# PSUM and probability tiles of two banks for both heads and for two GLA token tiles, in a two-layer hybrid encoder

## The chip, the cores and the metric

The kernel runs on one core of one Trainium2 chip. The metric is the device time of one execution in microseconds (us): 1145.85 is the median of three runs of the kernel before (1144.88 to 1146.09). Everything is float32 or the same numbers in the rounded form fp32r. The five engines of the core work side by side, each through its own list of instructions in order: TensorE (PE) multiplies matrices into PSUM, VectorE (DVE) and ScalarE (ACT) work on SBUF and PSUM, GpSimd (POOL) on a few tiles, and SyncE (SP) issues the DMAs. PSUM has eight banks; one bank holds 512 float32 columns on 128 partitions.

## The reference

512 tokens of width 1024 pass through two layers. Each layer normalizes, multiplies by one wide input projection, and divides its columns among three mixers: gated linear attention (GLA, 4 heads), a convolution module with 31 taps, and attention with a bias (6 heads of 64). Their outputs are concatenated, projected and added; then comes an MLP with a squared ReLU. Cut to what matters here:

```python
kv = jnp.einsum('bnchk,bnchv->bnhkv', k_dec, vf)      # GLA, one product per chunk of 64
def step(state, inp):
    a, kv_c = inp
    state = a[..., None] * state + kv_c
    return state, state
_, states = lax.scan(step, init, (chunk_decay, kv))   # 8 chunks in sequence
o = jnp.einsum('bnchk,nbhkv->bnchv', qf, states)
o = o * lax.rsqrt(jnp.mean(o * o, axis=-1, keepdims=True) + EPS)
...
scores = einsum('bnqhd,bnkhd->bnhqk', qc, k_band) * (ATT_HEAD_DIM ** -0.5)
p = jax.nn.softmax(jnp.where(valid, scores + bias, NEG_INF), axis=-1)
o = einsum('bnhqk,bnkhd->bnqhd', p, v_band)
...
h = h + mixed @ w_out[l]
h = h + sq_relu_mlp(rmsnorm(h, norm_ffn[l]), w_up[l], w_down[l])
```

## The kernel before

Activations lie transposed: 128 of the 1024 features on the partitions, 512 tokens along the free axis. Each operand of a large product is split in two fp32r numbers, high and low, and each product is three matmuls (lines 165 to 167): high by high, high by low, low by high. The weights arrive by DMA as float32; ACT makes the high part (L126), DVE the low part (L127).

A layer runs as follows. First the convolution's three projections `cv`, then the group `in_0`. Then comes a list of units (near line 803): projections of attention's queries and keys (`in_3` to `in_8`), of GLA's queries (`in_1`, `in_2`), and three token groups `tb`, `ta`, `tc` in which the tokens lie on the partitions (lines 465 to 467). After each unit's pieces, which count as so many microseconds of products, the table PACE advances three side tasks by a rate: attention (`att_steps`), GLA (`gla_steps`) and the convolution. The side tasks are generators; each `yield` is a step. Next is the output projection in two parts (`op`), beside the first of which attention and GLA go on; then the MLP (`up`, `dn`). So the order of the program text, and a scheduler's choice by priority, sets where a side task's matmuls stand between the dense ones on PE.

Attention works on pairs of heads. For head pair `pr` the steps are: scores of query tiles 0 and 1, scores of tile 2, transposes of 0 and 1, scores of 3, transposes of 2, values of 0 and 1, transposes of 3, values of 2 and 3. The scores (`sc`, L679) of each head have their own PSUM bank of the tag "at" (three buffers): head `s` uses rows 64·s to 64·s + 63 of the array. `softmax` adds the bias and takes the maximum on DVE (`mx`, L692), then the exponential and the scaling on ACT, into the probability tile `sn`. `turn` transposes `sn` on PE (`pt`, L711), into another bank of "at", and ACT copies it to `ps`. `values` multiplies it with the values (`ao`, L722), 64 columns of the array for each head, also in "at". The projections `in_3` and `in_4` and small norms take "at" too.

```python
BANKS = {"mm": 3, "at": 3, "gc": 2}
for step, *idx in (
    (scores, (0, 1)), (scores, (2,)), (turns, 0, 1), (scores, (3,)), (turns, 2),
    (attended, 0, 1), (turns, 3), (attended, 2, 3),
):
```

GLA and the convolution share the tag "gc" (two banks). `gz` (L501) and `gx` make the gates; `kv` (L544) is the product of keys and values for two token tiles, 64 rows by 64 columns of the array for each; DVE carries the state on from chunk to chunk (`st`); `go` (L583) multiplies the queries by the states, for one token tile at a time; ACT copies it out, DVE normalizes it, and `gla_out` transposes it (`ot`, L621).

## Time and profile before

| | |
|---|---|
| median of three runs | 1145.85 us (1144.88 to 1146.09) |
| the profiled execution | 1146.69 us |
| its span, from first to last instruction | 1144.9 us |
| busy of the span: PE, its weight loads, DVE, ACT, POOL | 99%, 81%, 55%, 43%, 2% |
| mean granted clock of PE | 0.997 |
| read from HBM | 105.22 MB |

The profiled execution is longer than its span by 1.8 us, which lie around it. The profile's times are of this one execution. The start and the busy time of each instruction are shown by the timeline; the matmuls of a pipelined engine overlap there, so that the distance from one start to the next, not a matmul's own duration, tells what it occupies. A plain float32 matmul such as `go` or `kv` stands there as two, so x16 are eight of the program.

### The profile page before, as it was taken

What the parts mean: (1) busy time and instruction counts of PE and PEld (TensorE: products, weight loads), DVE (VectorE), ACT (ScalarE), POOL (GpSimd) and SP (SyncE); (2) the same over time, 40 slices, a digit from 0 to 9 for tenths busy, and PEclk for the clock granted to TensorE, in tenths of its full rate; (3) what the DMA queues carried; (4) which work ended last, traced back from release to release, by engine and by line L of the source; (5) the groups of instructions that cost most, each with busy time, mean ns of one, the idle gap of its engine ahead of it and who ended that gap; (6) DMA issues with size and microseconds to landing.
All of it is one profiled execution on the core that took longest, in us unless ns stands there. A gap on an engine that the chain in (4) does not pass through costs nothing.

```text
span 1144.9 us, 14044 instructions
## 1 busy us (share of the span) xinstructions
PE 1131.3 (99%) x5552; PEld 929.5 (81%) x5552; DVE 628.2 (55%) x1041; ACT 488.8 (43%) x843; POOL 20.9 (2%) x39
## 2 busy tenths in 40 slices
PE   9999999999999999999999999999999999999996
PEld 7888878888888888888888788788888888888885
DVE  7897786743433344334359957867434333443344
ACT  6454795634311243333243567845343112433222
POOL 0000010000000000000000000100000000000002
PEclk9999999999999999999999999999999999999998
DMA  8231312232223223332242321222332232223312
GB/s 282 94 106 51 97 56 74 95 106 94 92 92 109 94 92 94 107 112 81 77 132 90 104 60 38 93 74 92 103 100 92 92 105 97 92 93 99 104 37 74
DMA packets 34657, 108.21 MB, mean 95 GB/s; under 512 B 4256, under 2 KB 7456, under 8 KB 34592
## 3 DMA queue, kind: packets, MB, share of 16 engines
q1 hardware_dynamic: 34592, 107.33, 28.9%
q8 instruction: 43, 0.70, 0.3%
q14 instruction: 22, 0.18, 0.0%
HBM read 105.22 MB, written 2.10 MB: 94 GB/s over the span
## 4 chain that ended last, share of the span: by engine, by line
PE 97%; DVE 1%; DMA 1%; ACT 0%; issue 0%; DVEq 0%; SPq 0%; ACTq 0%
PE dn L167 10%; PE dn L166 10%; PE dn L165 10%; PE up L166 10%; PE up L165 10%; PE up L167 10%; PE in L165 3%; PE op L165 3%; PE op L166 3%; PE in L167 3%; PE in L166 3%; PE op L167 3%; PE sc L679 2%; PE ao L722 1%; PE pt L711 1%; PE cv L165 1%
## 5 line engine op out<-in xcount | busy, mean ns | idle before, releaser
L126 ACT CAST h_w<-r_w 128x1024 fp32r<-128x1024 f32 x146 | 153.8, 1053 | 443.8 <-PE dn L166 216.8
L127 DVE TENSOR_TENSOR l_w<-r_w,h_w 128x1024 fp32r<-128x1024 f32 x146 | 178.4, 1223 | 300.2 <-ACT h_w L126 299.4
L165 PE MATMUL dn<-uh,h_w 128*128 128x512 f32 (+1 forms) x528 | 202.7, 384 | 0.0
L167 PE MATMUL dn<-uh,l_w 128*128 128x512 f32 (+1 forms) x528 | 202.5, 383 | 0.0
L166 PE MATMUL dn<-ul,h_w 128*128 128x512 f32 (+1 forms) x528 | 202.4, 383 | 0.0
L166 PEld LDWEIGHTS dn<-ul,h_w 128*128 128x128 f32 x528 | 99.2, 188 | 20.0
L165 PEld LDWEIGHTS dn<-uh,h_w 128*128 128x128 f32 x528 | 99.2, 188 | 19.9
L167 PEld LDWEIGHTS dn<-uh,l_w 128*128 128x128 f32 x528 | 99.2, 188 | 19.8
L872 DVE TENSOR_TENSOR dt<-dn,n2r 128x512 f32<-128x512 f32 (+1 forms) x33 | 22.3, 675 | 115.0 <-PE dn L167 115.0
L382 DVE SCALAR_TENSOR_TENSOR acc<-hp,cl,acc 128x512 f32<-128x512 f32 x120 | 82.1, 745 | 0.1
L862 DVE TENSOR_TENSOR ul<-ur,uh 128x512 fp32r<-128x512 f32 x64 | 44.4, 693 | 2.1
L857 ACT ACTIVATE ur<-ur 128x512 f32<-128x512 f32 x64 | 40.6, 634 | 1.9
L856 ACT ACTIVATE ur<-up 128x512 f32<-128x512 f32 x64 | 37.8, 590 | 0.0
L697 ACT ACTIVATE sn<-sn,mx 128x128 f32<-128x128 f32 (+3 forms) x48 | 26.6, 554 | 9.7 <-DVE mx L692 9.4
L702 ACT ACTIVATE sn<-sn,ri 128x128 f32<-128x128 f32 (+3 forms) x48 | 26.8, 559 | 6.4 <-DVE ri L701 6.2
L861 DVE CAST uh<-ur 128x512 fp32r<-128x512 f32 x64 | 27.3, 427 | 0.0
L793 DVE TENSOR_TENSOR hT<-hT,op 128x512 f32<-128x512 f32 x32 | 21.9, 683 | 6.4 <-PE op L167 6.2
L167 PE MATMUL up<-x_0h,l_w 128*128 128x512 f32 x64 | 24.9, 389 | 0.0
L165 PE MATMUL up<-x_2h,h_w 128*128 128x512 f32 x64 | 24.9, 389 | 0.0
L165 PE MATMUL up<-x_0h,h_w 128*128 128x512 f32 x64 | 24.9, 389 | 0.0
L166 PE MATMUL up<-x_0l,h_w 128*128 128x512 f32 x64 | 24.9, 389 | 0.0
L165 PE MATMUL up<-x_1h,h_w 128*128 128x512 f32 x64 | 24.9, 389 | 0.0
(814 smaller groups left out, 2387.3 us busy)
## 6 DMA issues: line engine op xcount, KB each, us to landing
r_w<-in_wm SPq DMA_DIRECT2D x146, 512.0 KB, 3.5
r_wo<-in_wo SPq DMA_DIRECT2D x16, 512.0 KB, 3.6
r_tb<-in_wtb SPq DMA_DIRECT2D x8, 480.0 KB, 4.2
r_ta<-in_wta SPq DMA_DIRECT2D x8, 480.0 KB, 4.3
ab<-in_relx SPq DMA_DIRECT2D x12, 256.0 KB, 4.3
r_tc<-in_wtc SPq DMA_DIRECT2D x8, 384.0 KB, 3.3
r_wc<-in_wc SPq DMA_DIRECT2D x6, 384.0 KB, 4.6
hT<-in_xT SPq DMA_DIRECT2D x8, 256.0 KB, 5.5
```

What stands on the lines that cost most here:

```text
L126: nc.scalar.copy(out=hi, in_=raw)
L127: nc.vector.tensor_tensor(out=lo, in0=raw, in1=hi.bitcast(F32), op=ALU.subtract)
L165: nc.tensor.matmul(out=ps, lhsT=hi[:, sl], rhs=xh, start=first and i == 0, stop=False)
L166: nc.tensor.matmul(out=ps, lhsT=hi[:, sl], rhs=xl, start=False, stop=False)
L167: nc.tensor.matmul(out=ps, lhsT=lo[:, sl], rhs=xh, start=False, stop=last and i == n - 1)
L382: nc.vector.scalar_tensor_tensor(out=acc[c], in0=hp[c][:, j : j + T], scalar=weight(c, j), in1=acc[c], op0=ALU.mult, op1=ALU.add,)
L697: nc.scalar.activation(out=sn[:, 0:n], in_=sn[:, 0:n], func=AF.Exp, scale=-1.0, bias=mx, accum_out=sm)
L702: nc.scalar.activation(out=sn[:, 0:n], in_=sn[:, 0:n], func=AF.Copy, scale=ri)
L856: nc.scalar.activation(out=r, in_=ps, func=AF.Relu)
L857: nc.scalar.activation(out=r, in_=r, func=AF.Square)
L861: nc.vector.tensor_copy(out=hi, in_=r)
L862: nc.vector.tensor_tensor(out=lo, in0=r, in1=hi.bitcast(F32), op=ALU.subtract)
```

## The change

Scores, transposes and probabilities of both heads of a pair now share tiles of two banks, [128, 2, 512]: one PSUM buffer "at" of two banks in place of three of one, in SBUF two tiles each for `sn` and `ps` in place of five. `ao` gets a bank of its own, which `in_0` uses too. `in_3` and `in_4` are the two banks of one tile `in_34`. "gc" becomes one buffer of two banks. Copies of transposes take both heads, and for query tiles 0 and 1 all four parts, in one ACT instruction. GLA works on two token tiles at a time: the states of four chunks, then sixteen matmuls `go`, then one normalization of both and six transposes into one tile. Two rates of PACE differ. In the MLP the pairs `uh`, `ul` that lived in `sn` and `ps` tiles lie in one such tile. The diff, cut to its core:

```diff
-BANKS = {"mm": 3, "at": 3, "gc": 2}
+ROOM = {"s": 38, "cv": 8, "sn": 2, "ps": 2, "bias": 4, "os": 3}
+BANKS = {"mm": 3, "ao": 1, "at": 1, "gc": 1}
...
-    (0.4, 0.75, 0.6),
-    (0.3, 0.35),
+    (0.4, 0.65, 0.6),
+    (0.3, 0.2),
...
-    def at_ps(name):
-        return mm_ps(name, "at")
+    def two_heads(name, pool=pp, tag="at", dt=F32):
+
+        return pool.tile([P, 2, T], dt, tag=tag, bufs=(BANKS if pool is pp else ROOM)[tag], name=name)
 
     def gc_ps(name):
-        return mm_ps(name, "gc")
+        return two_heads(name, tag="gc")[:, 0, :]
...
-        psb.append(in_group(0, at_ps))
+        psb.append(in_group(0, lambda name: mm_ps(name, "ao")))
...
-                pk = [gc_ps(f"kv{l}_{i}_{h}") for h in range(2)]
+                pk = two_heads(f"kv{l}_{i}", tag="gc")
...
-            for t in range(NT):
-                if t % 2 == 0:
-                    kvs = chunk_products(t // 2)
...
+            for i in range(2):
+                kvs = chunk_products(i)
+                yield True
                 sts = []
-                for h in range(2):
-                    n = 2 * t + h
-                    pk = kvs[h]
-                    c0 = 2 * (t % 2) * GDV
-                    cur = sp.tile([P, 2 * GDV], F32, tag="st", bufs=4, name=f"st{l}_{n}")
+                for n in range(4 * i, 4 * i + 4):
+                    pk = kvs[:, n % 2, (n // 2 % 2) * 2 * GDV :]
...
-                o = s_tile(f"os{l}_{t}")
-                ov = o[:, 0:384].rearrange("p (a b d) -> p a b d", b=2, d=GDV)
-                pos = [gc_ps(f"go{l}_{t}_{hh}") for hh in range(2)]
-                for pr in range(2):
-                    for hh in range(2):
-                        rr = slice(hh * GP, (hh + 1) * GP)
-                        for h in range(2):
-                            n = 2 * t + h
-                            nc.tensor.matmul(
-                                out=pos[hh][h * CHUNK : (h + 1) * CHUNK, pr * GDV : (pr + 1) * GDV],
-                                lhsT=qT[pr][rr, n * CHUNK : (n + 1) * CHUNK],
-                                rhs=sts[h][rr, pr * GDV : (pr + 1) * GDV], start=True, stop=True,
-                            )
-                for hh in range(2):
+                yield True
+                o = sp.tile([P, 2, 384], F32, tag="os", bufs=ROOM["os"], name=f"os{l}_{i}")
+                go = two_heads(f"go{l}_{i}", tag="gc")
+                for t in range(2):
+                    for pr in range(2):
+                        c0 = (2 * t + pr) * GDV
+                        for hh in range(2):
+                            rr = slice(hh * GP, (hh + 1) * GP)
+                            for h in range(2):
+                                n = 4 * i + 2 * t + h
+                                nc.tensor.matmul(
+                                    out=go[h * CHUNK : (h + 1) * CHUNK, hh, c0 : c0 + GDV],
+                                    lhsT=qT[pr][rr, n * CHUNK : (n + 1) * CHUNK],
+                                    rhs=sts[2 * t + h][rr, pr * GDV : (pr + 1) * GDV],
+                                    start=True, stop=True,
+                                )
+                for t in range(2):
                     nc.scalar.copy(
...
-                sq = s_tile(f"oq{l}_{t}")
-                nc.scalar.activation(out=sq[:, 0:384], in_=o[:, 0:384], func=AF.Square)
-                vs = small([P, GH], f"ov{l}_{t}")
+                flat = o.rearrange("p t d -> p (t d)")
+                sq = sp.tile([P, 2 * 384], F32, tag="os", bufs=ROOM["os"], name=f"oq{l}_{i}")
+                nc.scalar.activation(out=sq, in_=flat, func=AF.Square)
+                vs = small([P, 2 * GH], f"ov{l}_{i}")
                 nc.vector.reduce_sum(
-                    out=vs, in_=sq[:, 0:384].rearrange("p (h d) -> p h d", d=GDV), axis=AX.X
+                    out=vs, in_=sq.rearrange("p (h d) -> p h d", d=GDV), axis=AX.X
                 )
...
-        def gla_out(o_s, t):
-            o = o_s[t]
-            nc.vector.tensor_tensor(
-                out=o[:, 0:384], in0=o[:, 0:384], in1=gates[t][:, 0:384], op=ALU.mult
-            )
-            pt = gc_ps(f"ot{l}_{t}")
-            for f in range(3):
-                nc.tensor.transpose(
-                    out=pt[:, f * P : (f + 1) * P], in_=o[:, f * P : (f + 1) * P], identity=ident
-                )
-            ts = slice(t * P, (t + 1) * P)
-            if t == 0:
+        def gla_out(o_s, i):
+            o = o_s[i]
...
+            for j in range(2):
+                t = 2 * i + j
+                nc.vector.tensor_tensor(
+                    out=o[:, j, :], in0=o[:, j, :], in1=gates[t][:, 0:384], op=ALU.mult
+                )
+                for f in range(3):
+                    fc = slice(f * P, (f + 1) * P)
+                    nc.tensor.transpose(out=pt[:, j, fc], in_=o[:, j, fc], identity=ident)
+            ts = slice(2 * i * P, 2 * (i + 1) * P)
...
             for f, (hi, lo) in enumerate(gmx):
-                src = pt[:, f * P : (f + 1) * P]
-                nc.scalar.copy(out=hi[:, ts], in_=src)
-                nc.vector.tensor_tensor(
-                    out=lo[:, ts], in0=src, in1=hi.bitcast(F32)[:, ts], op=ALU.subtract
-                )
+                src = pt[:, :, f * P : (f + 1) * P]
+                hi3, lo3 = (a[:, ts].rearrange("p (j t) -> p j t", t=P) for a in (hi, lo))
+                nc.scalar.copy(out=hi3, in_=src)
+                nc.vector.tensor_tensor(out=lo3, in0=src, in1=hi3.bitcast(F32), op=ALU.subtract)
```

```diff
@@ attention
-                pss = [at_ps(f"sc{l}_{2 * pr + s}_{idx[0]}") for s in range(2)]
+                pss = two_heads(f"sc{l}_{pr}_{idx[0]}")
+                probs[idx[-1]] = two_heads(f"sn{l}_{pr}_{idx[0]}", sp, "sn")
...
                     for s in range(2):
-                        softmax(i, s, pss[s][:, (i - idx[0]) * 2 * P :])
-
-            def softmax(i, s, psc):
+                        softmax(i, s, pss[:, s, (i - idx[0]) * 2 * P :], probs[idx[-1]][:, s, (i - idx[0]) * P :])
+
+            def softmax(i, s, psc, sn):
...
-            def turn(i, s):
-                n = (i + 1) * P
-                nm_ = f"{l}_{2 * pr + s}_{i}"
-                sn = probs[i, s]
-                pt = at_ps(f"pt{nm_}")
-                for j in range(i + 1):
-                    nc.tensor.transpose(
-                        out=pt[:, j * P : (j + 1) * P], in_=sn[:, j * P : (j + 1) * P], identity=ident
-                    )
-                p_ = room("ps", i, s)
-                nc.scalar.copy(out=p_[:, 0:n], in_=pt[:, 0:n])
-                pts[i, s] = p_
+
+            def turns(*idx):
+                nm_ = f"{l}_{pr}_{idx[0]}"
+                sn = probs[idx[-1]]
+                pt = two_heads(f"pt{nm_}")
+                n = 0
+                for i in idx:
+                    for s in range(2):
+                        for j in range(i + 1):
+                            cc = slice(n + j * P, n + (j + 1) * P)
+                            nc.tensor.transpose(out=pt[:, s, cc], in_=sn[:, s, cc], identity=ident)
+                    n += (i + 1) * P
+                p_ = two_heads(f"ps{nm_}", sp, "ps")
+                nc.scalar.copy(out=p_[:, :, 0:n], in_=pt[:, :, 0:n])
+                at = 0
+                for i in idx:
+                    pts[i] = p_[:, :, at * P : (at + i + 1) * P]
+                    at += i + 1
...
-                    pos.append(at_ps(f"ao{l}_{pr}"))
+                    pos.append(mm_ps(f"ao{l}_{pr}", "ao"))
...
+            both = two_heads(f"in{l}_34") if pr == 0 else None
             for i in range(2):
                 yield from in_pieces(
-                    3 + 2 * pr + i, lambda ps: att_evac(pr, i, ps), at_ps if pr == 0 else mm_ps
+                    3 + 2 * pr + i, lambda ps: att_evac(pr, i, ps),
+                    mm_ps if pr else lambda name: both[:, i, :],
...
-                tags = places[i]
-                hi = s_tile(f"uh{l}_{f}", F32R, tags)
-                lo = s_tile(f"ul{l}_{f}", F32R, tags)
+                if places[i] in ("sn", "ps"):
+                    both = two_heads(f"uhl{l}_{f}", sp, places[i], F32R)
+                    hi, lo = both[:, 0, :], both[:, 1, :]
+                else:
+                    hi = s_tile(f"uh{l}_{f}", F32R, places[i])
+                    lo = s_tile(f"ul{l}_{f}", F32R, places[i])
```

How this changes the order on PE, at three places of the first layer (line numbers are each kernel's own).

PE, from the projection `in_3` (weights `h_w_3`, `l_w_3`) on, before and after; `tb0p` is the first tile of the token group `tb`.

```order
L166 MATMUL in_3_368<-x_7l,h_w_3_363 128x512
L167 MATMUL in_3_368<-x_7h,l_w_3_364 128x512
L165 MATMUL in_4_411<-x_0h,h_w_4_406 128x512
L166 MATMUL in_4_411<-x_0l,h_w_4_406 128x512
L167 MATMUL in_4_411<-x_0h,l_w_4_407 128x512
L165 MATMUL in_4_411<-x_1h,h_w_4_406 128x512
```

```order
L167 MATMUL in_34_362<-x_7l,h_w_3_364 128x512
L168 MATMUL in_34_362<-x_7h,l_w_3_365 128x512
L466 MATMUL tb0p_467<-h_tb_0_444,x_0h 128x480
L467 MATMUL tb0p_467<-l_tb_0_445,x_0h 128x480
...
L467 MATMUL tb0p_467<-l_tb_1_451,x_2h 128x480
L468 MATMUL tb0p_467<-h_tb_1_450,x_2l 128x480
L166 MATMUL in_34_362<-x_0h,h_w_4_406 128x512
L167 MATMUL in_34_362<-x_0l,h_w_4_406 128x512
```

Before, `in_4` follows at once, in another bank; after, nine matmuls of `tb` stand between the two halves of `in_34`.

PE, where the scores of query tile 2 of the first head pair stand; `sc_0_2` and `sc_1_2` are heads 0 and 1 before, and `sc_0_2` is both heads after.

```order
L167 MATMUL in_6_700<-x_5h,l_w_6_696 128x512
L679 MATMUL sc_0_2_721<-qk_0_1h,qk_0_0h 128x384
L679 MATMUL sc_1_2_722<-qk_0_1h,qk_0_0h 128x384
L679 MATMUL sc_0_2_721<-qk_0_1h,qk_0_0l 128x384
L679 MATMUL sc_1_2_722<-qk_0_1h,qk_0_0l 128x384
L679 MATMUL sc_0_2_721<-qk_0_1l,qk_0_0h 128x384
L679 MATMUL sc_1_2_722<-qk_0_1l,qk_0_0h 128x384
L165 MATMUL in_6_700<-x_6h,h_w_6_695 128x512
```

```order
L168 MATMUL in_6_696<-x_7h,l_w_6_692 128x512
L166 MATMUL in_1_759<-x_0h,h_w_1_754 128x512
L167 MATMUL in_1_759<-x_0l,h_w_1_754 128x512
L675 MATMUL sc_0_2_717<-qk_0_1h,qk_0_0h 128x384 x2
L675 MATMUL sc_0_2_717<-qk_0_1h,qk_0_0l 128x384 x2
L675 MATMUL sc_0_2_717<-qk_0_1l,qk_0_0h 128x384 x2
L168 MATMUL in_1_759<-x_0h,l_w_1_755 128x512
```

The group moved from before `in_6`'s sixth matmul from the end to behind the second of the next projection, `in_1`: eight dense matmuls later.

PE, the last `go` of the layer, before (beside the scores of heads 4 and 5) and after; `st` are the states, `gq` the queries.

```order
L167 MATMUL op_0_0_1813<-mc_1h,l_wo_0_0_1809 128x512
L679 MATMUL sc_4_3_1827<-qk_2_1h,qk_2_0h 128x512
L679 MATMUL sc_4_3_1827<-qk_2_1h,qk_2_0l 128x512
L679 MATMUL sc_4_3_1827<-qk_2_1l,qk_2_0h 128x512
L583 MATMUL go_3_0_1858<-st_6_1851,gq_0_809 64x96
L583 MATMUL go_3_0_1858<-st_7_1854,gq_0_809 64x96
L583 MATMUL go_3_1_1859<-st_6_1851,gq_0_809 64x96
L679 MATMUL sc_5_3_1828<-qk_2_1h,qk_2_0h 128x512
L679 MATMUL sc_5_3_1828<-qk_2_1h,qk_2_0l 128x512
L679 MATMUL sc_5_3_1828<-qk_2_1l,qk_2_0h 128x512
L583 MATMUL go_3_1_1859<-st_7_1854,gq_0_809 64x96
L583 MATMUL go_3_0_1858<-st_6_1851,gq_1_848 64x96
```

```order
L466 MATMUL tc0p_1673<-h_tc_2_1334,x_4h 128x384
L582 MATMUL go_1_1681<-st_4_1661,gq_0_797 64x96
L582 MATMUL go_1_1681<-st_5_1664,gq_0_797 64x96
L582 MATMUL go_1_1681<-st_4_1661,gq_0_797 64x96
L582 MATMUL go_1_1681<-st_5_1664,gq_0_797 64x96
...
L582 MATMUL go_1_1681<-st_6_1667,gq_0_797 64x96
L582 MATMUL go_1_1681<-st_7_1670,gq_0_797 64x96
...
L582 MATMUL go_1_1681<-st_7_1670,gq_1_836 64x96
L467 MATMUL tc0p_1673<-l_tc_2_1335,x_4h 128x384
```

Before, the eight matmuls of token tile 3 are cut by the scores of head 5, and those of tile 2 stand in two places ahead of them. After, sixteen matmuls of token tiles 2 and 3 are one run among dense matmuls of `tc`.

## Rows read from the trace of the kernel before

**Rows 1.** The page, busy time: us, share of the span, instructions, by engine.

```profile
PE 1131.3 (99%) x5552; PEld 929.5 (81%) x5552; DVE 628.2 (55%) x1041; ACT 488.8 (43%) x843; POOL 20.9 (2%) x39
```

**Rows 2.** The page, the chain that ended last, share by engine.

```profile
PE 97%; DVE 1%; DMA 1%; ACT 0%; issue 0%; DVEq 0%; SPq 0%; ACTq 0%
```

**Rows 3.** Stretches: us, busy us (instructions) of PE, PEld, DVE, ACT, POOL; PEclk, DMA share, GB/s.

```profile
28.00:112.00 84.00, 84.00 (x423) 68.81 (x423) 72.36 (x121) 41.34 (x79) 1.10 (x5) 1.00 0.27 88
112.00:172.00 60.00, 60.00 (x443) 47.69 (x442) 46.51 (x120) 50.29 (x121) 3.02 (x3) 1.00 0.23 74
674.00:734.00 60.00, 60.00 (x443) 47.69 (x441) 46.67 (x120) 50.45 (x121) 3.02 (x3) 1.00 0.22 73
1120.00:1145.00 25.00, 13.69 (x105) 12.65 (x103) 12.44 (x22) 6.84 (x16) 7.40 (x9) 0.84 0.25 84
```

**Rows 4.** Timeline, PE, dense products: start, us, engine, line, operation, out<-in, count [wait].

```profile
36.90 0.39 PE L167 MATMUL in<-x_7h,l_w 128*128 128x512 f32 x1
37.13 0.39 PE L165 MATMUL in<-x_0h,h_w 128*128 128x512 f32 x1
```

**Rows 5.** Timeline, PE: a run of scores among dense products.

```profile
68.74 0.39 PE L167 MATMUL in<-x_7h,l_w 128*128 128x512 f32 x1
...
69.64 0.28 PE L679 MATMUL sc<-qk_1h,qk_0l 64*128 64x256 f32 x2
69.76 0.28 PE L679 MATMUL sc<-qk_1l,qk_0h 64*128 64x256 f32 x2
...
70.30 0.40 PE L166 MATMUL in<-x_0l,h_w 128*128 128x512 f32 x1
```

**Rows 6.** Timeline, PE: a run of `go` of x16.

```profile
151.59 0.44 PE L467 MATMUL tc0p<-h_tc,x_7l 128*128 128x384 f32 x1
151.96 0.56 PE L583 MATMUL go<-st,gq 64*64 64x96 f32 x16
...
152.73 0.34 PE L466 MATMUL tc0p<-l_tc,x_0h 128*128 128x384 f32 x1
```

**Rows 7.** Timeline, PE: a run of `go` of x8.

```profile
162.50 0.33 PE L467 MATMUL tc0p<-h_tc,x_3l 128*128 128x384 f32 x1
...
162.85 0.34 PE L466 MATMUL tc0p<-l_tc,x_4h 128*128 128x384 f32 x1
163.12 0.55 PE L583 MATMUL go<-st,gq 64*64 64x96 f32 x8
...
163.88 0.33 PE L465 MATMUL tc0p<-h_tc,x_5h 128*128 128x384 f32 x1
```

**Rows 8.** Timeline, PE: `go` inside a group of scores.

```profile
169.34 0.40 PE L167 MATMUL op<-mc_1h,l_wo 128*128 128x512 f32 x1
...
170.56 0.39 PE L583 MATMUL go<-st,gq 64*64 64x96 f32 x6
...
171.77 0.54 PE L583 MATMUL go<-st,gq 64*64 64x96 f32 x10
...
172.58 0.40 PE L166 MATMUL op<-ma_0l,h_wo 128*128 128x512 f32 x1
```

**Rows 9.** Timeline, DVE: it reads the product `in_3`.

```profile
38.33 0.68 DVE L649 SCALAR_TENSOR_TENSOR aq<-in,n_0rb 128x512 f32<-128x512 f32 x1
```

**Rows 10.** Timeline, PE, second layer: the scores wait for DVE.

```profile
635.19 0.44 PE L679 MATMUL sc<-qk_1h,qk_0h 64*128 64x384 f32 x1
636.20 0.41 PE L679 MATMUL sc<-qk_1h,qk_0h 64*128 64x384 f32 x1 [0.57 <-DVE mx L692]
```

**Rows 11.** Timeline, DVE: the last maximum of the second head pair's first group.

```profile
120.12 0.08 DVE L692 DVE_READ_ACCUMULATOR2_ANT mx<- 128x1 f32 x1
```

**Rows 12.** Timeline, PE: `gz` beside it.

```profile
119.63 0.92 PE L501 MATMUL gz<-wg,gq 128*128 128x256 f32 x3
```

**Rows 13.** Timeline, PE, near the start.

```profile
9.61 0.63 PE L165 MATMUL cv<-x_1h,h_wc 128*128 128x512 f32 x1
10.04 0.63 PE L166 MATMUL cv<-x_1l,h_wc 128*128 128x512 f32 x1
```

More of the change, by code (lines that the diff above doesn't have):

```diff
@@ L169, in col_sums @@
     def col_sums(src, name, w=ones):
-        pc = at_ps(f"{name}pc")
+        pc = gc_ps(f"{name}pc")
         for j in range(NT):
@@ L204, in bcast @@
             )
-        pb = at_ps(f"{name}pb")
+        pb = gc_ps(f"{name}pb")
         nc.tensor.matmul(out=pb, lhsT=ones, rhs=dg, start=True, stop=True)
@@ L253, in encoder_kernel @@
     nc.vector.tensor_copy(out=ones_r, in_=ones)
-    warm = at_ps("warm")
+    warm = gc_ps("warm")
     for i in range(NWARM):
@@ L544, in chunk_products @@
                                 nc.tensor.matmul(
-                                    out=pk[h][hh * GP : (hh + 1) * GP, c0 : c0 + GDV],
+                                    out=pk[hh * GP : (hh + 1) * GP, h, c0 : c0 + GDV],
                                     lhsT=kd[i][rows, o0 : o0 + GP],
@@ L551, in gla_states @@
             prev = None
-            for t in range(NT):
-                if t % 2 == 0:
-                    kvs = chunk_products(t // 2)
-                    yield True
+            for i in range(2):
+                kvs = chunk_products(i)
+                yield True
                 sts = []
-                for h in range(2):
-                    n = 2 * t + h
-                    pk = kvs[h]
-                    c0 = 2 * (t % 2) * GDV
-                    cur = sp.tile([P, 2 * GDV], F32, tag="st", bufs=4, name=f"st{l}_{n}")
+                for n in range(4 * i, 4 * i + 4):
+                    pk = kvs[:, n % 2, (n // 2 % 2) * 2 * GDV :]
+                    cur = sp.tile([P, 2 * GDV], F32, tag="st", bufs=6, name=f"st{l}_{n}")
                     if n == 0:
@@ L604, in gla_states @@
                 yield True
-                r = rsqrt(GH, f"on{l}_{t}", v=vs)
-                for g in range(GH):
-                    gc = slice(g * GDV, (g + 1) * GDV)
+                r = rsqrt(2 * GH, f"on{l}_{i}", v=vs)
+                for g in range(2 * GH):
+                    gc = slice((g % GH) * GDV, (g % GH + 1) * GDV)
                     nc.vector.scalar_tensor_tensor(
-                        out=o[:, gc], in0=o[:, gc], scalar=r[:, g : g + 1], in1=gn[:, gc],
-                        op0=ALU.mult, op1=ALU.mult,
+                        out=o[:, g // GH, gc], in0=o[:, g // GH, gc], scalar=r[:, g : g + 1],
+                        in1=gn[:, gc], op0=ALU.mult, op1=ALU.mult,
@@ L626, in gla_out @@
                 gmx.extend(
-                    tuple(s_tile(f"gm{l}_{f}{i}", F32R) for i in range(2)) for f in range(3)
+                    tuple(s_tile(f"gm{l}_{f}{h}", F32R) for h in range(2)) for f in range(3)
                 )
             for f, (hi, lo) in enumerate(gmx):
-                src = pt[:, f * P : (f + 1) * P]
-                nc.scalar.copy(out=hi[:, ts], in_=src)
-                nc.vector.tensor_tensor(
-                    out=lo[:, ts], in0=src, in1=hi.bitcast(F32)[:, ts], op=ALU.subtract
-                )
+                src = pt[:, :, f * P : (f + 1) * P]
@@ L658, in att_pair @@
             bias = biases[pr]
-            probs, pts, shared = {}, {}, {}
-            def room(kind, i, s):
-                key = (kind, "b" if i == 1 else (s, i // 3))
-                if key not in shared:
-                    shared[key] = s_tile(f"{kind}{l}_{2 * pr + s}_{i}", tag=kind)
-                c0 = (0, 2 * P * s, P, 0)[i]
-                return shared[key][:, c0 : c0 + (i + 1) * P]
+            probs, pts = {}, {}
             def scores(idx):
-                pss = [at_ps(f"sc{l}_{2 * pr + s}_{idx[0]}") for s in range(2)]
+                pss = two_heads(f"sc{l}_{pr}_{idx[0]}")
+                probs[idx[-1]] = two_heads(f"sn{l}_{pr}_{idx[0]}", sp, "sn")
                 for i in idx:
@@ L679, in scores @@
                             nc.tensor.matmul(
-                                out=pss[s][:, c0 : c0 + nk], lhsT=q[rows, qc], rhs=k[rows, 0:nk],
+                                out=pss[:, s, c0 : c0 + nk], lhsT=q[rows, qc], rhs=k[rows, 0:nk],
                                 start=t == 0, stop=t == 2,
@@ L724, in values @@
                             lhsT=av[j][:, h * AD : (h + 1) * AD],
-                            rhs=pts[i, s][:, j * P : (j + 1) * P],
+                            rhs=pts[i][:, s, j * P : (j + 1) * P],
                             start=j == 0, stop=j == i,
                         )
-            def turns(*idx):
-                for i in idx:
-                    for s in range(2):
-                        turn(i, s)
             def attended(*idx):
                 if not pos:
-                    pos.append(at_ps(f"ao{l}_{pr}"))
+                    pos.append(mm_ps(f"ao{l}_{pr}", "ao"))
                 for i in idx:
@@ L770, in gla_steps @@
             yield from gla_states(kd, decs[0], o_s)
-            for t in range(NT):
-                gla_out(o_s, t)
+            for i in range(2):
+                gla_out(o_s, i)
                 yield True
```

18 lines of the change are left out of this document (9 added, 9 removed).

## The prediction

> **What bounds the kernel now.** I read the page first: TensorE (PE) is busy 1131.3 of 1144.9 us [rows 1], and the chain that ended last runs through PE for 97% of the span [rows 2]. Then the busy time by stretch [rows 3]. 11.3 of the 13.6 idle microseconds lie in the last 25 us (25.00 − 13.69), which the change doesn't touch. Between 112 and 172 us, where most of attention and gated linear attention (GLA) runs, PE is busy for all 60.00 us. The second layer (674 to 734) repeats this with the same 443 matmuls and the same busy times within 0.4%, so I price one layer and double it. VectorE (DVE) is the next engine: 72.36 of 84 us between 28 and 112, 46.51 of 60 after that. So time falls only if PE's own occupation falls, and it rises if PE must wait for DVE.
>
> "Busy" does not mean that PE streams columns. The timeline shows what it costs to go from one kind of matmul to another. Dense 512-column matmuls follow each other after 0.23 us (36.90 to 37.13) [rows 4], and of 384 columns after 0.175 (162.50 to 162.85 are two) [rows 7]. The scores, `sc`, use half of the array's rows, the products `ao` half of its columns, `kv` and `go` a quarter. Between 68.74 and 70.30 one run of scores stands among dense matmuls [rows 5]: 1.56 us, of which two dense pitches are 0.45 and six pairs of scores 6 × 0.12 = 0.70 (69.64 to 69.76). The other 0.41 us is spent in going into the other shape and out of it: **0.20 us for each change of shape**.
>
> **The change part by part.** Both programs issue the same matrix products, with the same columns. What differs is how often PE changes its shape: by the order of instructions 110 times before and 72 after, 19 fewer in each layer.
>
> 1. `go` in two runs of two token tiles instead of pieces: 13 changes become 4, 9 fewer. One of the pieces cuts a group of scores: between 169.34 and 172.58, `sc`, `go`, `sc`, `go` [rows 8], 5 changes where the scores alone have 2.
> 2. `ao` of the second head pair in one visit instead of three: 4 fewer.
> 3. The second `kv` no longer falls between the two heads of a group of scores: 2 fewer.
> 4. The second `gx` no longer falls into scores that it cut twice: 4 fewer.
>
> *Changes of shape:* 2 × 19 × 0.20 = 7.6 us.
>
> *Heads together:* two heads use different rows of the array, and as neighbours share the time: the pairs above take 0.12 for 2 × 256 columns. In two groups of each layer (those cut by `go` and by `kv`) the heads stand apart, so that three matmuls of 512 and three of 384 columns run alone. Together again they save 3 × 0.23 + 3 × 0.175 = 1.2 us a layer, 2.4 in both. Check on the first: 5 × 0.20 + 6 × 0.23 + 0.39 for `go` is 2.77, and rows 8 show 3.24 − 0.45 = 2.79.
>
> *Longer runs of `go`:* a plain-f32 `go` stands twice in the trace. A run of x8 costs 0.68 us (162.85 to 163.88, less two pitches) [rows 7], one of x16 only 0.79 (151.59 to 152.73, less two) [rows 6]. Less two changes that is 0.28 and 0.39, so the second eight cost 0.11. In a layer four runs of x8, one of x16 and the pieces x6 and x10 (some 0.55) take 2.06 us; two runs of x32 would take 2 × (0.39 + 2 × 0.11) = 1.2 if the 0.11 holds on, 1.56 if x32 costs twice x16. So 0.5 to 0.84 is saved, in which the lower end is the nearer to a row; I take 0.6 a layer, 1.2 in all.
>
> *Transposes* (`pt`, `ot`) in fewer visits: they keep the dense shape, so 0 to 0.3 a layer; I take 0.3 for both layers.
>
> Changing the array's shape empties it, by the Trainium skill ("TensorEngine Tiling (Array Packing)", section "Tiling Modes", key properties); by that rule alone merged transposes gain nothing, and the sum would be 0.3 smaller.
>
> Sum of gains: 7.6 + 2.4 + 1.2 + 0.3 = 11.5 us. Pricing the four kinds of visits by their measured extents instead of by terms gave me 12.2, so 10.5 to 13.5 are its bounds.
>
> *Fewer instructions elsewhere:* ACT has 62 fewer and DVE 32 fewer (copies and small operations for two heads or tiles at once). PE waits for neither in rows 3, so this is worth 0 unless DVE becomes the bound. The SBUF tiles (`s` from 41 to 38, `sn`, `ps` and `os` apart) change no order in the MLP: 0. PACE delays some GLA steps past attention steps; that is how the merged runs come about, and is priced with them.
>
> **What the change adds: waits.** Before, the attention tag "at" has three one-bank buffers; now one two-bank buffer is handed from scores to transposes to the next scores, and the GLA tag "gc" is likewise single. PE executes in order, so whatever is behind a waiting matmul waits too: dense projections, then their evacuations on DVE and ACT, then the following weight tile's casts.
>
> - The second half of the first projection pair (`in_4`) now waits until DVE has read the first (`in_3`). Nine `tb0p` matmuls are put between. The read ends at 38.33 + 0.68 = 39.01 [rows 9]; `in_4` would come to 37.13 + 9 × 0.22 = 39.11. Cost 0; without the nine it would be 1.9 us a layer.
> - `sc_0_2` waits for the maxima of both heads' first group. The second layer shows such a wait already: the first matmul at 635.19, the next after DVE's `mx` at 636.20, 1.0 us where one pitch was due [rows 10]. In the new order this group comes eight dense matmuls later and needs one more maximum: no change.
> - `sc_1_2` needs the last maximum at 120.12 + 0.08 = 120.20 [rows 11]; in the new order it comes after `gz` (119.63 here) [rows 12], at about 119.9. Cost 0.3 in each layer, 0.6 in both.
> - The other handovers (first transposes after the scores, their copies, `gx`, `lnm`, `go` after its states) arrive within 0.1 to 0.3 us of their producer; I give them 0.3 in all.
>
> So 0.9 us. Bounds: −0.2 (the wait in the second layer shortens) to 5.4, which is 0.3 at each of the 18 handovers that DVE releases (three for a head pair, three pairs, two layers).
>
> **Sum:** −11.5 + 0.9 = −10.6, and with the middle of the two ways of pricing (−11.9 + 0.9) −11.0. The profiled execution takes 1146.69 us, so 1135.7; it lies 0.84 above the median of 1145.85, so the median to expect is about 1135.
>
> **The rivals.**
>
> *Part is given back* (−2.3 to −8 us): 3 to 9 us of waits appear at the handovers. For it: DVE is busy 86% between 28 and 112 us, and a queue of taps of 0.7 us stands ahead of each maximum. Against it: those taps were there before, and most of the gain lies after 112 us, where DVE is at 78%. By the upper bound of 5.4 the time is 1145.85 − 11.9 + 5.4 = 1139.4.
>
> *Nothing* (within ±2.3): the visits' cost sits in PE's own clock and not in the shape, so that fewer changes gain nothing, or DVE's 86% is the real bound and PE only looks busy. Against it: the 0.41 us of rows 5 is start-to-start time on an engine that is never idle. 1145.
>
> *Slower, the single buffer:* each of the 18 handovers waits 1.0 us, as the one of rows 10 does. Then −11.9 + 18.0 = +6, 1152. It decides from 11.9/18 = 0.66 us for each. For it: with three buffers that wait occurred once in the trace of before, with less slack it could be the rule. Against it: the new order puts dense matmuls between almost all of them.
>
> *The clock.* Before about 10.5 us 512 columns take 0.43 us (9.61 to 10.04) [rows 13], the 1.2 GHz level; after that 0.23, the 2.4 GHz level, and the granted clock is 1.00 in all middle stretches of rows 3. If PE paused at each handover and fell back, a stretch at the low level would cost half its length, and some 24 us of it would eat the gain: 1146 or more. The Trainium skill ("TensorE: Matmul & The Clock Gate", section "A second HAM failure mode: psum-queue depth-cycling") tells of a kernel in which short pauses between matmul groups on changing PSUM banks made the clock swing. The trace of before has such pauses without a fall, so I give it little.
>
> **How the numbers follow.** A measurement of this kernel tells 0.2%, 2.3 us, from no change. The forecast (−8 to −14, its own range 1132 to 1138) 0.68; part given back 0.16; nothing 0.07; the single buffer's waits 0.07; the clock 0.02. So faster 0.84, same 0.07, slower 0.09. The range runs from the largest gain (13.5 + 0.8 for longer `go` runs, 1131.5) through three quarters of the second case, to 1142.
>
> **What would show it.** Changes of shape: in the stretch 112 to 190 no `sc` row stands between `go`, `kv` or `gx` rows; `go` stands as two runs of x32, each about 1.0 to 1.2 us start to start; the op stage begins some 5 us earlier in the first layer and the MLP at twice that in the second. Waits: the list of PE's waits still holds under 3 us for `sc`, `pt`, `in` and `go` together. The forecast is wrong if that list grows to over 5 us, if the granted clock of a middle stretch falls under 1.00, or if runs between shapes keep their 0.2 us but the dense pitch rises.

## The result, and the profile after

The changed kernel takes 1137.68 us (median of 6 runs, 1137.27 to 1138.29) against 1145.97 of the kernel before (6 runs, 1144.88 to 1146.35): a ratio of 0.993, interval [0.992, 0.994], or 8.3 us less. Forecast were 1135 and 11 us, with a range of 1131.5 to 1142.

The page of the kernel after, busy time and the shares of the chain that ended last; it answers to [rows 1, 2]:

```profile
PE 1119.6 (99%) x5552; PEld 923.9 (81%) x5552; DVE 623.5 (55%) x1009; ACT 483.0 (42%) x781; POOL 20.4 (2%) x39
PE 93%; ACT 3%; DVE 2%; issue 1%; DMA 0%; DVEq 0%; SPq 0%; ACTq 0%
```

TensorE (PE) has the same 5552 instructions and 11.7 us less of busy time, but the span fell by 8.4 (1144.9 to 1136.5). So PE's idle time grew by 3.3 us, which shows in the chain too: PE's share of it fell from 97% to 93%, and ACT, DVE and "issue" (time in which an engine waits for nothing that the profile shows) have those 4%. The stretches of [rows 3], as windows of the same length that lie like those of before (us, busy us of PE, PEld, DVE, ACT, POOL, granted clock, DMA share, GB/s):

```profile
112.00:172.00 60.00, 58.49 (x461) 48.52 (x459) 47.34 (x115) 50.16 (x108) 3.41 (x3) 1.00 0.26 82
668.00:728.00 60.00, 58.48 (x458) 48.79 (x457) 45.88 (x114) 49.39 (x108) 3.40 (x3) 1.00 0.26 81
1112.00:1137.00 25.00, 13.71 (x105) 12.66 (x103) 12.43 (x22) 6.84 (x16) 7.41 (x9) 0.84 0.25 84
```

Between 112 and 172 us PE now fits 461 matmuls instead of 443, and stands idle for 1.5 us, where it never did before. The last 25 us are as before, and the granted clock of the two middle stretches is 1.00, as before. What PE waits for, in all of the kernel after (us in total, times, longest):

```profile
PE go L582 <- DVE st L565: 1.5, 2, 0.8
PE nf256pb L272 <- ACT nf256sq L269: 1.4, 1, 1.4
PE cv L166 <- ACT h_wc L127: 1.1, 1, 1.1
PE warm L257 <- DVE eps L253: 1.1, 1, 1.1
PE pt L708 <- DVE mx L687: 0.9, 2, 0.4
PE sc L675 <- DVE mx L687: 0.8, 2, 0.4
```

The first, fifth and sixth line are of the change: 3.2 us, one wait of each kind in each layer (before there was one wait of `sc` for DVE in all, that of [rows 10]). The other three lie at the start and the end. This list counts only the idle time that the record shows; start-to-start distances show more, since a wait can also hide in a step that the record counts as busy. The timeline of PE after, around those waits in the first layer:

```profile
143.04 1.04 PE L708 MATMUL pt<-kc,sn 128*128 128x128 f32 x8
144.00 0.89 PE L582 MATMUL go<-st,gq 64*64 64x96 f32 x32
144.82 0.44 PE L466 MATMUL tc0p<-h_tc,x_2h 128*128 128x384 f32 x1
...
158.16 0.34 PE L466 MATMUL tc0p<-h_tc,x_4h 128*128 128x384 f32 x1
159.25 0.89 PE L582 MATMUL go<-st,gq 64*64 64x96 f32 x32 [0.76 <-DVE st L565]
...
161.76 0.34 PE L467 MATMUL tc0p<-l_tc,x_7h 128*128 128x384 f32 x1
162.49 0.44 PE L675 MATMUL sc<-qk_1h,qk_0h 64*128 64x384 f32 x2 [0.39 <-DVE mx L687]
...
178.03 0.40 PE L168 MATMUL op<-mc_1h,l_wo 128*128 128x512 f32 x1
178.88 0.87 PE L708 MATMUL pt<-kc,sn 128*128 128x128 f32 x6 [0.45 <-DVE mx L687]
179.51 0.48 PE L166 MATMUL op<-ma_0h,h_wo 128*128 128x512 f32 x1
```

And DVE after, in front of two of them:

```profile
158.57 0.53 DVE L565 SCALAR_TENSOR_TENSOR st<-st,dec,kv 128x96 f32<-128x96 f32 x2
...
176.24 1.91 DVE L611 SCALAR_TENSOR_TENSOR os<-os,on_1r,gn 128x96 f32<-128x96 f32 x8
...
178.15 0.67 DVE L687 CUSTOM_DVE_ANT_0 sn<-sc,ab 128x512 f32<-128x512 f32 x1
178.75 0.08 DVE L687 DVE_READ_ACCUMULATOR2_ANT mx<- 128x1 f32 x1
```

The first `go` of x32 waits for nothing and runs from 144.00 to 144.82. The second starts at 159.25 after a wait of 0.76 us, since DVE ends the last state at 158.57 + 0.53 = 159.10. The transposes at 178.88 wait for a maximum that DVE ends at 178.83; ahead of it DVE normalizes both token tiles in eight instructions of 1.91 us. A visit is a stretch of PE in which it works on something else than dense products. Above what the same visit costs where it waits for nothing, the waits of the first layer come to 0.82 (`go`), 0.47 (`sc` at 162.49), 0.36 and 0.68 (`pt` at 168.13 and 178.88): 2.33 us. Three smaller ones stand in no list: `pt` at 80.53 (0.17), `sc` at 120.13 (0.17) and `pt` at 123.78 (0.33) start within 0.15 us of the end of a maximum on DVE. With them it is 3.0 us in the first layer, and 3.1 in the second.

The wait of the second layer's `sc` [rows 10] is gone; PE after, at the same place:

```profile
633.13 0.39 PE L167 MATMUL in<-x_0l,h_w 128*128 128x512 f32 x1
633.45 0.44 PE L675 MATMUL sc<-qk_1h,qk_0h 64*128 64x384 f32 x2
```

What TensorE's own work gained can be read from the rows. From each step of PE, one start to the next, take off the pitch of a dense matmul of as many columns (0.227, 0.218 and 0.174 us for 512, 480 and 384), and add up what is left in the visits: in the first layer (28 to 226 us) 42.8 us before and 39.7 after, in the second (588 to 790) 43.8 and 39.8. Without the waits on either side that is 6.1 us less in each layer, **12.3 us in both**, of which the new waits take 6.1 back, while the old wait's end gives 1.0. This makes 7.2 of the 8.4 us of the span. The other 1.2 lie outside the visits: 0.5 in the dense steps of the same stretches, 0.3 before 28 us, 0.4 behind the start of the last matmul.

### The profile page after: what moved, and what is told of

The parts are those of the page before. It is cut to its first block, busy times and chain, and to the rows that moved or that the text cites. A ratio compares the mean times of both kernels' runs of the same rounds, so it can differ in the third digit from the quotient of the medians.

```text
span 1136.5 us, 13937 instructions
## 1 busy us (share of the span) xinstructions
PE 1119.6 (99%) x5552; PEld 923.9 (81%) x5552; DVE 623.5 (55%) x1009; ACT 483.0 (42%) x781; POOL 20.4 (2%) x39
## 4 chain that ended last, share of the span: by engine, by line
PE 93%; ACT 3%; DVE 2%; issue 1%; DMA 0%; DVEq 0%; SPq 0%; ACTq 0%
PE dn L168 10%; PE dn L167 10%; PE dn L166 10%; PE up L168 10%; PE up L167 10%; PE up L166 10%; PE in L166 3%; PE in L168 3%; PE in L167 3%; PE op L166 2%; PE op L168 2%; PE op L167 2%; PE ao L721 1%; PE pt L708 1%; PE cv L166 1%; PE cv L167 1%
## 5 line engine op out<-in xcount | busy, mean ns | idle before, releaser
L166 PE MATMUL dn<-uh,h_w 128*128 128x512 f32 (+1 forms) x396 | 152.0, 384 | 0.0
L167 PE MATMUL dn<-ul,h_w 128*128 128x512 f32 (+1 forms) x396 | 151.7, 383 | 0.0
L168 PE MATMUL dn<-uh,l_w 128*128 128x512 f32 (+1 forms) x396 | 151.6, 383 | 0.0
L166 PEld LDWEIGHTS dn<-uh,h_w 128*128 128x128 f32 x396 | 74.4, 188 | 15.1
L167 PEld LDWEIGHTS dn<-ul,h_w 128*128 128x128 f32 x396 | 74.4, 188 | 14.8
L168 PEld LDWEIGHTS dn<-uh,l_w 128*128 128x128 f32 x396 | 74.4, 188 | 14.6
L168 PE MATMUL dn<-uhl,l_w 128*128 128x512 f32 (+1 forms) x132 | 50.9, 385 | 0.0
L166 PE MATMUL dn<-uhl,h_w 128*128 128x512 f32 (+1 forms) x132 | 50.8, 385 | 0.0
L167 PE MATMUL dn<-uhl,h_w 128*128 128x512 f32 (+1 forms) x132 | 50.7, 384 | 0.0
L167 PEld LDWEIGHTS dn<-uhl,h_w 128*128 128x128 f32 x132 | 24.8, 188 | 5.1
L168 PEld LDWEIGHTS dn<-uhl,l_w 128*128 128x128 f32 x132 | 24.8, 188 | 5.1
L166 PEld LDWEIGHTS dn<-uhl,h_w 128*128 128x128 f32 x132 | 24.8, 188 | 4.8
```

Source lines behind the costliest of these rows:

```text
L166: nc.tensor.matmul(out=ps, lhsT=hi[:, sl], rhs=xh, start=first and i == 0, stop=False)
L167: nc.tensor.matmul(out=ps, lhsT=hi[:, sl], rhs=xl, start=False, stop=False)
L168: nc.tensor.matmul(out=ps, lhsT=lo[:, sl], rhs=xh, start=False, stop=last and i == n - 1)
```

## The experiments

The theory: each change of the array's shape costs TensorE 0.20 us, and 38 fewer of them (72 for 110, in the order and in the traces), with groups of scores no longer cut, make the gain; waits at the single two-bank buffer and for `go`'s states take part of it back. The rivals: fewer instructions on ScalarE and VectorE make the gain; or the waits come from elsewhere than the buffer.

**The price of a shape, by itself (e1, e2).** In the middle of 60 products of the MLP, where no side task runs on TensorE, one extra matmul whose result nobody uses:

```diff
-                group(ps, w, x2, range(KT), True, True)
+                group(ps, w, x2, range(KT // 2), True, False)
+                if i > 0:
+                    pd = two_heads(f"pd{l}_{f}")
+                    nc.tensor.matmul(
+                        out=pd[:, 0, 0:256], lhsT=w[0][0:64, 0:P], rhs=x2[0][0][0:64, 0:256],
+                        start=True, stop=True,
+                    )
+                group(ps, tuple(a[:, KT // 2 * P :] for a in w), x2, range(KT // 2, KT), False, True)
```

e2 has `0:P` in place of the two `0:64`.

> The changed kernel with 60 extra matmuls whose results nobody uses, one in the middle of each 'up' product of the MLP but the first of each half, 64 rows of the array x 256 columns: a stretch without side work on TensorE. Shape theory (0.20 us of TensorE for each change of the array's shape): 60 x 0.113 us for the columns + 120 x 0.20 = 6.8 + 24 = 30.8 us over the changed kernel's 1137.7, so about 1168. Rival (a change of shape is free, the gain came from fewer instructions on ScalarE and VectorE): 6.8 over, 1144.5, the same as the kernel with 128 rows.

> The same 60 extra matmuls of 256 columns with all 128 rows, which keep the dense shape. Both theories: 60 x 0.113 = 6.8 us over the changed kernel, about 1144.5. The difference to the kernel with 64 rows, over 120, is the price of one change of shape: 0.20 by the shape theory, 0 by the rival.

Measured: 1169.06 us (1.0203 of before, [1.019, 1.0216]) and 1146.07 (1.0004, [0.9995, 1.0013]). The difference of 22.99 us over 120 changes is **0.192 us for each change**. The extra matmul itself cost (1146.07 − 1137.68)/60 = 0.14 us, not 0.113. The timeline of PE, first with 64 rows, then with 128:

```profile
235.52 0.39 PE L168 MATMUL up<-x_3h,l_w 128*128 128x512 f32 x1
235.83 0.38 PE L838 MATMUL pd<-x_0h,h_w 64*128 64x256 f32 x1
236.15 0.50 PE L166 MATMUL up<-x_4h,h_w 128*128 128x512 f32 x1
236.48 0.40 PE L167 MATMUL up<-x_4l,h_w 128*128 128x512 f32 x1
```

```profile
234.88 0.39 PE L168 MATMUL up<-x_3h,l_w 128*128 128x512 f32 x1
235.10 0.28 PE L838 MATMUL pd<-x_0h,h_w 128*128 128x256 f32 x1
235.22 0.40 PE L166 MATMUL up<-x_4h,h_w 128*128 128x512 f32 x1
235.45 0.40 PE L167 MATMUL up<-x_4l,h_w 128*128 128x512 f32 x1
```

Three steps are longer: 0.31 us ahead of the matmul for 0.22, 0.32 behind it for 0.12, and 0.33 for 0.23 between the two dense ones that follow, 0.39 for the two changes. The rival, by which a change of shape is free, falls. 38 changes at 0.192 us are 7.3 of the 12.3 us.

**Each half alone (e4, e9).** e4 has the new GLA with the old attention (three one-bank buffers); e9 the new attention with the old GLA and old PACE. In short:

```diff
-BANKS = {"mm": 3, "ao": 1, "at": 1, "gc": 1}
+BANKS = {"mm": 3, "at": 3, "gc": 1}
```

That is e4, against the changed kernel; its `att_pair` and `qk_into` are those of before. e9, against the kernel of before, in short:

```diff
-BANKS = {"mm": 3, "at": 3, "gc": 2}
+BANKS = {"mm": 3, "ao": 1, "at": 1, "gc": 2}
```

Its `gla_states` and `gla_out` are those of before.

> Only the GLA part of the change and the new PACE: attention as before, with three one-bank buffers, ao among them, and copies per head. 82 changes of shape in the order (before 110, changed 72). Shape theory: 28 x 0.20 = 5.6 us, 1.2 for longer runs of go and some 2 for heads that stand together again: 8.8 less than before, 1137.2, with 10 x 0.20 = 2 us more than the changed kernel for the shapes and up to 3.3 us fewer waits of sc and pt if the single two-bank buffer causes these. If the waits come from VectorE's own queue they stay, and the time is about 1139.5. Rival (fewer instructions on ScalarE and VectorE): about half of the gain, 1141.8.

> Only the attention part of the change: two-bank tiles for scores, transposes and probabilities of both heads, ao in a bank of its own; GLA one token tile at a time with one-bank tiles, and the PACE of before. 96 changes of shape in the order (before 110, changed 72). Shape theory: 14 x 0.20 = 2.8 us, 2.4 for heads that are no longer cut apart, so 5.2 less without waits; the waits of sc and pt for VectorE's maxima in the third pair, 1.5 a layer, come with the single buffer: 3 more. So 1145.5 - 5.2 + 3 = about 1143.3, 1140.3 if the waits come only with the GLA part. Rival (the gain is the GLA part's alone): 1145.5 or more.

Measured: e4 1140.42 us (0.9955, [0.9941, 0.9969]), e9 1143.33 (0.9981, [0.9972, 0.999]). Against the kernel of before in their own rounds they bring 5.2 and 2.2 us alone, together 7.4, where the whole brings 8.3. What PE waits for DVE in e4:

```profile
PE sc L685 <- DVE mx L698: 1.0, 1, 1.0
```

and in e9:

```profile
PE sc L673 <- DVE mx L685: 2.0, 2, 1.0
PE pt L706 <- DVE mx L685: 0.6, 2, 0.3
```

With three buffers the waits of the third pair are absent: e4's one wait is that of the second layer's early scores. With the single buffer they are there even with the old GLA. So the buffer brings the waits of `sc` and `pt`; e9 was expected at 1143.3 with them, and came there. e4 was expected at 1137.2 by the shapes alone and was 3.2 above; 1.4 of that is its one wait as start-to-start distance (2.38 against 0.93 at that visit). The rest goes with the clock in part: of the two longest of its six runs (1141.87 and 1143.85 us) the mean granted clock is 0.993, of a third (1140.34) 0.995, and of every other run on record 0.996 or 0.997. The three at 0.996 took 1138.81, 1139.17 and 1140.50. Where the clock fell in the others stays open, since only the profile of the last of these was kept.

**The old PACE (e3).**

```diff
-    (0.4, 0.65, 0.6),
-    (0.3, 0.2),
+    (0.4, 0.75, 0.6),
+    (0.3, 0.35),
```

> The changed kernel with the two PACE rows of before (0.75 in place of 0.65, 0.35 in place of 0.2). The order then has 74 changes of shape (72), the second kv product stands six dense matmuls ahead of the third pair's first scores and so farther ahead of go. Wait theory: the wait of go for the states (0.84 us in each layer) falls away, 1.7 us, against 0.4 for two changes of shape: about 1136.4, unless sc or pt then wait more. Rival (the pace was what brought the merged runs): most of the gain is lost, 1142 or more.

Measured: 1137.98 us (0.9932, [0.992, 0.9944]), the same as the changed kernel. `go` still waited, 1.3 us in both layers, since it moved ahead with the states, and 1.0 us of waits of `ot` came in place of those of `pt`. So PACE is not what brought the gain, and the theory's 1136.4 was a miss.

**Maxima and states first (e5, e6).** `with tc.high_priority():` around the maxima (e5), and also around the states (e6):

```diff
-                nc.vector.tensor_tensor_reduce(
...
+                with tc.high_priority():
+                    nc.vector.tensor_tensor_reduce(
...
-                            nc.vector.scalar_tensor_tensor(
...
+                            with tc.high_priority():
+                                nc.vector.scalar_tensor_tensor(
```

> The changed kernel with a higher scheduling priority for VectorE's maxima of the scores, so that they stand ahead of the weights' low parts and other work in VectorE's list. 70 changes of shape (72). Theory (the single two-bank buffer makes TensorE wait for maxima that stand behind other work on VectorE: in each layer 0.45 for sc of the third pair's tile 2, 0.36 and 0.7 for pt, 0.15 for sc of the second pair): these fall to nearly nothing, 2 x 1.65 = 3.3 us, and 0.4 for two changes of shape less: about 1134. The wait of go for the states (0.84 in each layer) stays or moves. Rival (the waits come from the softmax chain itself, over ScalarE, or are replaced by waits for weights that VectorE now delivers later): within 1 us of the changed kernel, 1137 to 1138.5.

> The same higher priority for the maxima and for the states st of GLA. 72 changes of shape; go stands twelve dense matmuls earlier in the order after its states than with the maxima alone. Theory: the wait of go goes as well, 2 x 0.84 = 1.7 us more than the run with the maxima alone, less 0.4 for two changes of shape: about 1133. Rival (the order puts go earlier by as much as the states become earlier): the wait of go stays, 1134 to 1135.

Measured: e5 1137.68 us (0.9936, [0.9922, 0.9949]), e6 1136.40 (0.9923, [0.991, 0.9937]). Both expectations, 1134 and 1133, were missed: e5 came out at its rival's number, e6 above both of its numbers. e5's waits, then e6's (without those at the start and the end):

```profile
PE sc L675 <- DVE mx L688: 2.2, 2, 1.1
...
PE pt L709 <- DVE mx L688: 1.2, 3, 0.5
...
PE sc L675 <- ACT ps L712: 0.4, 1, 0.4
```

```profile
PE go L583 <- DVE st L566: 0.8, 2, 0.4
```

In e5 the wait of `go` went, and that of `sc` grew from 0.8 to 2.2: the scheduler put the next scores of the third pair eleven dense matmuls nearer to the first ones (24 between them for 35). In e6 they stand 22 farther off (46), and the listed waits fell from 3.2 us in the changed kernel to 0.8. It is the fastest kernel here; its interval overlaps that of the changed kernel, so that a gain of some 1 us is likely but not shown.

**A later `go` (e10).** The kernel of e6 with the GLA rates 0.6 and 0.25:

```diff
-    (0.4, 0.65, 0.6),
-    (0.3, 0.2),
+    (0.4, 0.6, 0.6),
+    (0.3, 0.25),
```

> The kernel with higher priority for maxima and states, and PACE's GLA rate 0.6 in place of 0.65 beside the last token group, 0.25 in place of 0.2 beside the output projection. 74 changes of shape (72); go stands 24 dense matmuls behind kv in place of 18, sc of the third pair's tile 2 six matmuls nearer to the first scores. Wait theory: go's wait of 0.47 in each layer goes, 0.9, less 0.4 for two changes: 1136.0, if sc doesn't wait instead. Rival (the scores, now nearer to the maxima they wait for, take the wait over): 1137 to 1138.

Measured: 1137.98 us (0.9928, [0.9914, 0.9942]): the rival's number; the theory's 1136.0 was a miss. PE in the third pair of the first layer:

```profile
159.72 0.34 PE L468 MATMUL tc0p<-h_tc,x_5l 128*128 128x384 f32 x1
159.99 0.89 PE L583 MATMUL go<-st,gq 64*64 64x96 f32 x32
160.81 0.44 PE L466 MATMUL tc0p<-h_tc,x_6h 128*128 128x384 f32 x1
161.09 0.34 PE L467 MATMUL tc0p<-l_tc,x_6h 128*128 128x384 f32 x1
...
164.05 0.44 PE L676 MATMUL sc<-qk_1h,qk_0h 64*128 64x384 f32 x2 [1.00 <-DVE mx L689]
```

`go` no longer waits, and the scores, six matmuls nearer to their maxima than in e6, wait 1.00 us instead.

**Heads apart within a group (e7).**

```diff
-                    for t, (q, k) in enumerate(((qh, kh), (ql, kh), (qh, kl))):
-                        for s in range(2):
+                    for s in range(2):
+                        for t, (q, k) in enumerate(((qh, kh), (ql, kh), (qh, kl))):
```

> The changed kernel with the three matmuls of one head's scores ahead of the three of the other in each group, in place of alternating heads: same shape, same columns, 72 changes of shape, but neighbours now use the same rows of the array. If neighbours in different rows share the time (0.12 us for 2 x 256 columns in the trace), half of the pairs now run alone: of 3 products x (256 + 256 + 384 + 512) columns for each head and pair, 25,344 columns in both layers, nearly all lose their partner (one of three products at the border keeps it), so 25,344 x 0.000443 = 11.2 us at most and two thirds of it, 7.5, at least: 1145 to 1149. Rival (the order of heads doesn't matter): 1137.7.

Measured: 1138.39 us (0.9938, [0.9925, 0.9952]): no loss; the expectation of 1145 to 1149 fell. PE of e7:

```profile
68.65 0.39 PE L675 MATMUL sc<-qk_1h,qk_0h 64*128 64x256 f32 x2
68.88 0.29 PE L675 MATMUL sc<-qk_1h,qk_0l 64*128 64x256 f32 x2
68.99 0.29 PE L675 MATMUL sc<-qk_1l,qk_0h 64*128 64x256 f32 x2
69.11 0.28 PE L675 MATMUL sc<-qk_1h,qk_0h 64*128 64x256 f32 x2
```

The program gives `hh, hl, lh` of one head and then `hh, hl, lh` of the other; the trace has them by twos, `hh` of both, `hl` of both. The second head's rows don't wait for the first head's three products. (The trace doesn't number the instructions; that the engine itself brings the two together is concluded from the program's list and these starts.) So two heads share the time when they stand in one run, in either order; what parted them before was another shape between them.

**Two copies (e8).**

```diff
-                nc.scalar.copy(out=p_[:, :, 0:n], in_=pt[:, :, 0:n])
+                for s in range(2):
+                    nc.scalar.copy(out=p_[:, s, 0:n], in_=pt[:, s, 0:n])
```

> The changed kernel with the copy of the transposes from PSUM undone to one ScalarE copy for each head: 18 more ScalarE instructions, same order on TensorE. Theory (the gain is TensorE's own, ScalarE has slack): within 0.5 us of the changed kernel, 1137.2 to 1138.2, or up to 1 us more where scores wait for the copy that frees the buffer. Rival (fewer instructions on ScalarE brought part of the gain): some 18 of the 94 instructions fewer on both engines, 18/94 x 8.3 = 1.6 us more, 1139.3.

Measured: 1139.31 us (0.9945, [0.9933, 0.9957]; runs from 1137.92 to 1140.24). The number is the rival's, but the rows show another cause. Rows of e8 in the second layer: the issue of a weight tile's DMA (SPq is the queue of SyncE), the tile's casts on ACT and DVE, and the scores on PE:

```profile
618.59 0.33 SPq L126 DMA_DIRECT2D r_w<-in_wm  x1
...
624.18 1.05 ACT L127 CAST h_w<-r_w 128x1024 fp32r<-128x1024 f32 x1 [3.19 <-DMA r_w<-in_wm]
...
625.27 1.23 DVE L128 TENSOR_TENSOR l_w<-r_w,h_w 128x1024 fp32r<-128x1024 f32 x1 [1.61 <-ACT h_w L127]
...
634.26 0.44 PE L675 MATMUL sc<-qk_1h,qk_0h 64*128 64x384 f32 x2 [1.60 <-DVE mx L687]
```

and the same weight tile in the changed kernel:

```profile
619.48 0.33 SPq L126 DMA_DIRECT2D r_w<-in_wm  x1
...
623.10 1.05 ACT L127 CAST h_w<-r_w 128x1024 fp32r<-128x1024 f32 x1 [1.22 <-DMA r_w<-in_wm]
```

In e8 this weight tile is issued 0.89 us earlier and is cast 1.08 us later, while PE is 0.85 ahead; DVE stands idle for 1.61 us, the maxima come later by that, and the scores wait 1.60 at the single buffer. This visit is 1.66 us longer than in the changed kernel (2.58 for 0.92); less the 0.85 that PE was ahead, that is most of the difference of the two profiled executions (1139.31 and 1138.29). Elsewhere the order and the waits are like the changed kernel's: the copies cost nothing there, and two of the five runs took 1137.92 and 1137.97, the changed kernel's time.

All twelve traces tell where this wait comes from. From issue to landing this one transfer takes 4.78 us in the kernel of before, 5.22 in e4 and 5.52 in e8, and 3.37 to 3.80 in the nine others; in just those three the scores wait here. Of the 143 such transfers behind 25 us, 0 to 5 in each trace take over 4.6 us, at changing places, also where both heads share a copy (three in e2 and in e6). So the wait of [rows 10] came from a transfer that took long. The three kernels have in common that each head is copied by itself, but no copy of the second layer stands ahead of this transfer (its first transposes come at 638.93 in e8), so chance is the nearer reading. What makes a transfer take long stays open. e8 undoes 18 of the 94 instructions that the change saves on ScalarE and VectorE; the others were not tried by themselves.

## Why the prediction was right, and where its terms were off

- *What bounds the kernel:* right. TensorE's own occupation fell, and the time with it; the granted clock stayed at 1.00 in the middle stretches, so the clock's rival falls. Neither trace shows a swing of the kind that the Trainium skill ("TensorE: Matmul & The Clock Gate", section "A second HAM failure mode: psum-queue depth-cycling") tells of, though PE now pauses between groups on changing banks (before there was one such pause, 0.57 us long [rows 10]).
- *Price of a change of shape:* 0.20 forecast, 0.192 measured by e1 and e2.
- *Longer `go`:* a run of x32 was put at 0.61 + 0.40 = 1.01 us beyond its dense neighbours if the cheap second eight holds on, and the 0.6 a layer that was taken means 1.13. Where it doesn't wait it costs 1.02 (e10: 159.72 to 161.09 is 1.37, less two pitches of 0.174). So the upper end came: 0.82 a layer, 1.6 in both for 1.2.
- *Heads together:* the size fits the rows but was not measured alone; its reason was only half right, since the heads must stand in one run of one shape, not as neighbours in the list (e7).
- *Sum of gains:* 11.9 forecast, 12.3 by the visits. 38 changes at 0.192 (7.3), the heads at the forecast's price (2.4) and `go` (1.6) make 11.3; the 1.0 that is left is for the transposes, put at 0.3, and for what no term names.
- *Waits:* the term that was mis-sized. "I give them 0.3 in all" for transposes, `go` after its states and the like: these alone, with `sc` of the third pair, are 5.7 us in both layers, and all new waits together 6.1, against 0.9 in the forecast; the list of `sc`, `pt` and `go` was to stay under 3 us and has 3.2. `in_4` cost nothing, as forecast (nine `tb0p` ahead, 38.80 in the trace after, no wait), and `sc_1_2` took 0.17 for 0.3. The step took arrival times from the trace of before, within 0.1 to 0.3 us of those producers; but TensorE arrives earlier by what it saved, and DVE has the states, the two-tile normalization and the output projection's weights ahead of the maxima.
- *Which case came:* by its waits, 5.1 us net, this is the rival *part is given back* (3 to 9 us of waits), which had 0.16. That the time still fell by 8.3, just inside the forecast's own −8 to −14, is partly luck: of the 8.4 us between the profiled executions 1.2 came from outside the visits, where the forecast had nothing, and 1.0 from the next term.
- *The second layer's wait* of 1.0 us was forecast to stay and went, as one transfer took 3.54 us for 4.78 (see e8).
- *Single buffer:* its rival asked for 0.66 us at each of 18 handovers. Twelve waited, 0.17 to 0.68 us, 4.4 in all or 0.25 on the average; the others didn't. The mechanism is there (e4, e9), the price isn't.
- *When the stages begin:* forecast some 5 us earlier at the output projection of the first layer; it was 2.2 (165.68 to 163.49), and 3.6 at the MLP's start (219.36 to 215.76); in the second layer the MLP began 7.9 us earlier (781.22 to 773.32), where some 10 were forecast.

## What to carry to other kernels

On a saturated TensorE, count how often the array's shape changes and read the price from start-to-start distances, since "busy" hides it: here 38 changes, the groups they cut and the longer runs were worth 12 us. A buffer that is shared by a chain of producers on two engines turns the other engine's queue into TensorE's wait, so price each handover with TensorE arriving earlier by what it saves. A wait taken away by the scheduler's own model can come back one step later, as in e5 and e10: compare all waits, not the one that was aimed at.

## What the runs showed of the hardware

- 0.192 us for each change between the full array and 64 rows, spread over three start-to-start steps, the last of them between two dense matmuls (e1, e2).
- Matmuls of the two 64-row halves, three of one half ahead of three of the other in the program, start as pairs in the trace and cost the same as alternating ones (1138.39 against 1137.68 us). The Trainium skill ("TensorEngine Tiling (Array Packing)", section "Tiling Modes") says that tiles run independently; e7 agrees, and by it this reaches at least over three products in the list.
- One 512 KB weight transfer took 3.37 to 3.80 us in nine traces and 4.78 to 5.52 in three, and in those three PE waited for it at second hand, through ACT, DVE and the buffer of the scores (1.60 us in e8).
